# A decoder layer on one core: both heads of a pair transposed in one group of six, their products with the values in the transposes' banks, and the low tiles of w_up 32 bytes further into larger buffers

## The chip, the cores and the metric

One NeuronCore of one Trainium2 chip runs the kernel. The metric is the device time of one execution in microseconds. Of the kernel before there are three such times, 434.8, 435.6 and 436.42, with 435.6 as the median, and one execution that was profiled. "TensorE" is the engine that multiplies matrices (PE in the profile), "VectorE" is DVE, "ScalarE" is ACT, "GpSimd" is POOL, and "SyncE" (SP) issues most of the transfers.

## The reference

One layer of a decoder on 256 rows of width 1024, in float32. One projection feeds three mixers. A keeps, for every query, the keys with the largest index scores and has 6 heads; B has 4 slots, each with three dilated windows that are merged by their softmax denominators; C is block-sparse attention with 6 heads (with 256 rows there is one block, so it is causal attention). Each mixer's output is projected, weighted by a sigmoid gate and summed; then follow an output projection, a layer norm, and a feed-forward part with squared relu beside a gated per-layer embedding (PLE):

```
proj = x @ w_in[i]
...
o_a = dsa_mixer(...)
o_b = dilated_mixer(...)
o_c = moba_mixer(...)
gates = jax.nn.sigmoid(x @ w_gate[i]).reshape(bsz, s_len, N_BRANCH, D_MODEL)
merged = (gates[:, :, 0] * (o_a @ w_br_a[i])
          + gates[:, :, 1] * (o_b @ w_br_b[i])
          + gates[:, :, 2] * (o_c @ w_br_c[i]))
x = layer_norm(ALPHA * x + merged @ w_out[i], ln1_g[i], ln1_b[i])
h = jnp.square(jax.nn.relu(x @ w_up[i])) @ w_down[i]
ple = jax.nn.sigmoid(x @ w_ple_gate[i]) * (p[i] @ w_ple[i])
x = layer_norm(ALPHA * x + h + ple, ln2_g[i], ln2_b[i])
```

## The kernel before

**Split operands.** [...] A product is then three matmuls: high by high, high by low, low by high (`prod`, L136). The class `Weights` streams the weights: SyncE loads a tile of 128 x 1024 into one of five `raw` buffers (L71), ScalarE copies it into a high tile `whi` (L75), and VectorE, for the early weights together with GpSimd, subtracts to get the low tile `wlo` (L79). A `raw` buffer is free for the next transfer when its subtraction is done. `W.get` runs up to four units ahead (`AHEAD`); `W.after` holds units back behind named instructions. Some units of w_out have their two parts in `hT` instead of `whi` and `wlo`.

**Stages of the run** (by the timeline): the index projections until 20 us; projections and the three mixers, B, then C, then A, until about 195; the merge (L570 to L575) and the output projection (`b<-whi,q`, `b<-hT,q`) until 225; the PLE products (`mm<-whi,ph`) until 231, and among them the first layer norm, LN1; the products with w_pg, the gate of PLE, until 256.5; w_up (L693 with the high tiles, L695 with the low ones, 32 units) until 346; w_down until 422, and a second layer norm.

**The mixers.** Heads are worked on in pairs: two pairs of slots in B, three pairs in C, three in A, 16 heads in all. For a pair, `logits` (L274) leaves the scores of two heads in two banks; `head` (or `slots` for B) adds the bias, takes the softmax (L346) and scales the rows (`scale_rows`, L335); `attend` transposes the probabilities of one head on TensorE in three blocks of 128 x 128 (L314) into a bank, splits them into `pt` (ScalarE L315, VectorE behind it), multiplies by the values (L318, L319) into another bank, and adds up four parts into `o`; `pair_out` splits `o` into `op`. Between these steps the list `TASKS` gives TensorE products of the gates (`mm<-xl,whi`, `mm<-xh,whi`, `mm<-xh,wlo`, 256 columns each), so that it has work while the other engines run the softmax.

**What sets the order.** The text of the program is not the order on the engines: a scheduler in the tile framework places each engine's instructions, with priorities and pools of buffers deciding. So an edit in one place can move instructions elsewhere. Every engine then executes its own list in order, and an instruction that waits holds up what is behind it. PSUM has banks: three for `mm`, and five (b0 to b4) that are handed out in fixed turns, by `ps_s` for scores (banks 0, 1, 2), `ps_t` for transposes (3), `ps_v` for the products with values (4), and `ps_a` for everything after.

**LN1.** `ln1` runs for two batches of 128 rows, b = 0 and 1, each in two halves of 512 columns: VectorE adds the residual (L634: `Y<-PL,b`), takes statistics (L611, `BN_STATS`; L616, L617), GpSimd takes the root (L618), VectorE normalizes (L623, L625), TensorE transposes four blocks (L644), and ScalarE (L646) and VectorE (L647) split the result into `x1`. The products with w_pg and w_up read `x1`. The PLE products go to `PL` by ScalarE (L663).

Of the kernel before, what the change touches and what calls it, by code (L numbers as in the profile page):

```python
# [11 lines left out]
F32 = mybir.dt.float32  # L12
F32R = mybir.dt.float32r
ALU = mybir.AluOpType
# [6 lines left out]
S = 256  # L21
# [20 lines left out]
FIRST = 4  # L42
DV = 640
# [6 lines left out]
class Weights:  # L50
# [6 lines left out]

    def add(self, src, n, hi=None, lo=None, stage=None, by="v", urgent=0):
        i = len(self.units)
        self.units.append((src, n, hi, lo, stage, by, urgent))  # L60
        return i

    def _split(self, i):
        nc = self.nc
        src, n, hi, lo, r, by, _ = self.units[i]
        if callable(src):
            r = src()
        else:
            if r is None:
                r = self.raw.tile([128, 1024], F32, name="raw", tag="raw")[:, :n]  # L70
            nc.sync.dma_start(r, src)  # L71
        if hi is None:
            hi = self.part.tile([128, 1024], F32R, name="whi", tag="whi")[:, :n]
            lo = self.part.tile([128, 1024], F32R, name="wlo", tag="wlo")[:, :n]
        nc.scalar.copy(hi, r)  # L75
        cut = ((nc.vector, slice(None)),) if by == "v" else (
            (nc.vector, slice(0, by * n // 1024)), (nc.gpsimd, slice(by * n // 1024, n)))
        for e, c in cut:
            low = e.tensor_tensor(lo[:, c], r[:, c], hi[:, c].bitcast(F32), op=ALU.subtract)  # L79
            if e is nc.gpsimd:  # L80
                self.pool = low.ins
        self.parts[i] = (hi, lo)

    def get(self, i, ahead=AHEAD):
        while self.done <= min(i + ahead, len(self.units) - 1):
            with ExitStack() as held:
                held.enter_context(self.tc.high_priority(offset=self.units[self.done][-1]))
                for ins in self.after:
                    held.enter_context(self.tc.issue_after(ins))
                self._split(self.done)  # L90
            self.done += 1
        return self.parts.pop(i)
# [3 lines left out]
def hybrid_layer(ctx: ExitStack, tc: tile.TileContext, x0, xn, pT, wqk, wva, wvb, wg, wbc, wba,  # L96
# [18 lines left out]

    ps_s, ps_t, ps_v, ps_a = turns((0, 1, 2)), turns((3,)), turns((4,)), turns((0, 1, 3, 2, 4))

# [44 lines left out]

    def add(*a):
        i = n_u[0]
        n_u[0] += 1
        return W.add(*a, by=DV if i < 58 else "v")

# [138 lines left out]
    n_pt = [0]  # L306

    def attend(P, vh, o, h):

        pt = pts[n_pt[0] % 2]  # L310
        n_pt[0] += 1
        t = next(ps_t)
        for c in range(3):
            pe.transpose(t[:, 128 * c:128 * c + 128], P[:, 128 * c:128 * c + 128], ident)  # L314
        act.copy(pt[:, 0], t[:, 0:384])  # L315
        dve.tensor_tensor(pt[:, 1], t[:, 0:384], pt[:, 0].bitcast(F32), op=ALU.subtract)
        v = next(ps_v).rearrange("p (a s) -> p a s", a=2)
        pe.matmul(v, lhsT=V[:, 0, vh], rhs=pt[:, :, 0:256], start=True, stop=False)  # L318
        pe.matmul(v[:, :, 128:256], lhsT=V[:, 1, vh], rhs=pt[:, :, 256:384], start=False,  # L319
                  stop=True)  # L320
        x = wk2.tile([64, 2, S], F32, name="ov", tag="ov")
        act.copy(x, v[64:128])
        dve.tensor_tensor(x, v[0:64], x, op=ALU.add)
        dve.tensor_tensor(o[64 * h:64 * h + 64], x[:, 0], x[:, 1], op=ALU.add)

# [11 lines left out]

    def head(s, t0, t1, vh, o, h):
        e = wk.tile([128, 384], F32, name="e", tag="e")
# [8 lines left out]
        scale_rows(e, den)  # L348
        attend(e, vh, o, h)

    def slots(qs, k, Ts, vh, o):
# [10 lines left out]
        for h in range(2):  # L362
# [9 lines left out]
            scale_rows(e[:, 0], den)  # L372
            attend(e[:, 0], vh + h, o, h)

# [11 lines left out]
    with ExitStack() as begin:  # L386
# [4 lines left out]
        with tc.high_priority(offset=1000):  # L391
# [4 lines left out]
            for k in range(KT):  # L396
# [5 lines left out]
                dve.tensor_tensor(sl[:, k], g0[:, k, S:], sh[:, k].bitcast(F32), op=ALU.subtract)  # L402
        first = [next(ps_s if f < 3 else ps_t)[:, 0:S] for f in range(FIRST)]
        for k in range(KT):
# [65 lines left out]
    for j in range(3):  # L470
        ps = feat(13 + 2 * j)
        k = k_pair(ps)
        q = q_pair(feat(14 + 2 * j))
        s = logits(q, k)
        o = opair()
        for h in range(2):
            n = 2 * j + h
            if n % 3 == 0:
                T = toeplitz(18 + n, 1)
            head(s, T[:, n % 3, 128:256], T[:, n % 3], 5 + n, o, h)  # L480
            fill("g")
        pair_out(o, 5 + j)
# [3 lines left out]
    T = None  # L486
    for j in range(3):
# [3 lines left out]
        for h in range(2):  # L491
# [4 lines left out]
            with tc.issue_after(W.pool):  # L496
                pool.tensor_tensor(ta[:, 0:128], T[:, n % 3, 128:256], am[:, 0:128], op=ALU.add)
                pool.tensor_tensor(ta[:, 128:384], T[:, n % 3], am[:, 128:384], op=ALU.add)
            head(s, ta[:, 0:128], ta[:, 128:384], 0, o, h)
            fill("gg" if n == 0 else "gc")  # L500
# [20 lines left out]
    u_pg = [add(wpg[i], 1024) for i in range(8)]  # L521
    u_up = [[add(wup[i], 1024)] for i in range(32)]

# [67 lines left out]
    w2 = ctx.enter_context(tc.tile_pool(name="w2", bufs=2, reuse_waits="tile"))  # L591
    s2 = ctx.enter_context(tc.tile_pool(name="s2", bufs=4, reuse_waits="tile"))
    Y = p3.tile([128, 2, D], F32, name="Y")
# [370 lines left out]
```

## Time and profile before

| | before |
|---|---|
| median of 3 runs | 435.6 us (434.8 to 436.42) |
| the profiled execution | 437.98 us |
| its span in the trace | 436.2 us |
| TensorE (PE) busy | 425.1 us, 97% of the span |
| VectorE (DVE) busy | 350.5 us, 80% |
| ScalarE (ACT) busy | 276.2 us, 63% |
| GpSimd (POOL) busy | 105.4 us, 24% |

The profile shows one execution. A row of a timeline gives the start in us from the span's beginning, the duration in us, the engine, the source line, the operation, what it writes and reads by the program's names, the shapes and how many alike were put together; in brackets stands the idle time ahead of it and what ended it. Matmuls overlap each other, so that the time from one start to the next, not the duration, is what one of them costs.

### The profile page before, as it was taken

To read this page: it belongs to the slowest core of one execution; us is meant where nothing else is said; L and a number is where in the kernel's file an instruction comes from. 1 tells how busy PE (TensorE), PEld (TensorE's weight loads), DVE (VectorE), ACT (ScalarE), POOL (GpSimd) and SP (SyncE) were. 2 spreads that over 40 slices of the span, in tenths; PEclk is the share of its full clock that TensorE was granted. 3 is DMA by queue.
4 is the path that set the end of the run, shared out by engine and by line. 5 is a ranking of instruction groups with operands and counts; after the bars stand their busy time and mean duration, and the time that the engine had idled before them with its cause. 6 is when DMAs were issued, how large, how long until landed. Compare 5 with 4: busy or idle time off the path is not lost.

```text
span 436.2 us, 7669 instructions
## 1 busy us (share of the span) xinstructions
PE 425.1 (97%) x2799; PEld 386.0 (88%) x2799; DVE 350.5 (80%) x625; ACT 276.2 (63%) x490; POOL 105.4 (24%) x98
## 2 busy tenths in 40 slices
PE   8999999999999999999998999999999999999993
PEld 8999999999999999999886888888888888888882
DVE  5978987577476577879957779999988897998984
ACT  6775375586787777756524567788887855665500
POOL 2563355395434566400000000000100000000001
PEclk9999999999999999999999999999999999999997
DMA  8797756457654436455960875656795377758411
GB/s 298 291 326 234 230 173 191 150 189 250 183 151 145 128 109 187 144 192 178 400 246 0 288 237 185 187 180 203 277 268 187 115 207 269 200 192 278 155 41 57
DMA packets 27690, 86.39 MB, mean 198 GB/s; under 512 B 2884, under 2 KB 6892, under 8 KB 27268
## 3 DMA queue, kind: packets, MB, share of 16 engines
q1 hardware_dynamic: 25872, 79.54, 55.1%
q0 software_dynamic: 640, 2.17, 2.9%
q10 hardware_dynamic: 1140, 4.19, 2.6%
q8 instruction: 22, 0.36, 0.3%
q14 instruction: 16, 0.13, 0.1%
HBM read 83.99 MB, written 1.90 MB: 197 GB/s over the span
## 4 chain that ended last, share of the span: by engine, by line
PE 88%; DVE 5%; issue 3%; DMA 2%; POOL 0%; POOLq 0%; ACT 0%; DVEq 0%; ACTq 0%
PE mm L136 40%; PE b L136 18%; PE mm L693 13%; PE mm L695 7%; PE b L274 3%; PE b L407 3%; DMA raw<-in_wpg_dram 2%; PE b L314 1%; PE b L318 1%; DVE hT L79 1%; DVE st L611 1%; DVE Y L625 1%; PE b L131 1%; DVE G L570 1%; DVE Y L634 1%
## 5 line engine op out<-in xcount | busy, mean ns | idle before, releaser
L79 DVE TENSOR_TENSOR wlo<-raw,whi 128x1024 fp32r<-128x1024 f32 (+5 forms) x146 | 157.5, 1092 | 41.9 <-ACT whi L75 37.9
L75 ACT CAST whi<-raw 128x1024 fp32r<-128x1024 f32 (+3 forms) x146 | 146.1, 1011 | 48.8 <-PE b L136 11.7
L79 POOL TENSOR_TENSOR wlo<-raw,whi 128x384 fp32r<-128x384 f32 (+3 forms) x58 | 78.8, 1367 | 82.6 <-ACT whi L75 73.6
L136 PE MATMUL mm<-xl,whi 128*128 128x256 f32 x336 | 95.7, 285 | 0.0
L136 PE MATMUL mm<-xh,whi 128*128 128x256 f32 x336 | 95.3, 284 | 0.0
L136 PE MATMUL mm<-xh,wlo 128*128 128x256 f32 x336 | 95.0, 283 | 0.0
L136 PEld LDWEIGHTS mm<-xl,whi 128*128 128x128 f32 x336 | 63.3, 188 | 1.0
L693 PE MATMUL mm<-x,whi 128*128 128x512 f32 x256 | 64.1, 392 | 0.0
L136 PEld LDWEIGHTS mm<-xh,whi 128*128 128x128 f32 x336 | 63.3, 188 | 0.7
L136 PEld LDWEIGHTS mm<-xh,wlo 128*128 128x128 f32 x336 | 63.3, 188 | 0.3
L693 PEld LDWEIGHTS mm<-x,whi 128*128 128x128 f32 x256 | 46.1, 189 | 8.3
L136 PE MATMUL b<-whi,hT 128*128 128x512 f32 (+2 forms) x164 | 51.8, 381 | 0.0
L695 PEld LDWEIGHTS mm<-x,wlo 128*128 128x128 f32 x256 | 34.9, 190 | 2.5
L741 POOL DMA_DIRECT2D rows<-in_wdq_dram x4 | 3.6, 972 | 135.3 <-DVE wlo L79 81.9
L695 PE MATMUL mm<-x,wlo 128*128 128x256 f32 x256 | 35.7, 282 | 0.0
L136 PEld LDWEIGHTS b<-whi,hT 128*128 128x128 f32 x164 | 30.5, 188 | 5.8
L136 PE MATMUL b<-wlo,hT 128*128 128x512 f32 (+2 forms) x82 | 31.2, 381 | 0.0
L618 POOL TENSOR_TENSOR rs<-rs,half 128x1 f32<-128x1 f32 x4 | 4.1, 1031 | 103.3 <-DVE rs L617 103.3
L698 DVE TENSOR_REDUCE r<-mm 128x256 f32<-128x512 f32 x32 | 22.0, 688 | 4.9 <-PE mm L695 4.9
L136 PE MATMUL mm<-op,whi 128*128 128x256 f32 x128 | 23.6, 281 | 0.0
L136 PE MATMUL b<-whi,x 128*128 128x512 f32 x64 | 20.4, 394 | 0.0
L241 ACT ACTIVATE G<-mm 128x256 f32<-128x256 f32 x24 | 9.2, 381 | 17.4 <-PE mm L136 17.3
(162 smaller groups left out, 740.0 us busy)
## 6 DMA issues: line engine op xcount, KB each, us to landing
raw<-in_wup_dram SPq DMA_DIRECT2D x32, 512.0 KB
raw<-in_wg_dram SPq DMA_DIRECT2D x24, 512.0 KB
raw<-in_wqk_dram SPq DMA_DIRECT2D x18, 512.0 KB
raw<-in_wdn_dram SPq DMA_DIRECT2D x16, 512.0 KB
raw<-in_wdq_dram SPq DMA_DIRECT2D x12, 512.0 KB
raw<-in_wout_dram SPq DMA_DIRECT2D x8, 512.0 KB
raw<-in_wpg_dram SPq DMA_DIRECT2D x8, 512.0 KB
T<-tabd SPq DMA_DIRECT2D x24, 128.0 KB
```

What stands on the lines that cost most here:

```text
L75: nc.scalar.copy(hi, r)
L79: low = e.tensor_tensor(lo[:, c], r[:, c], hi[:, c].bitcast(F32), op=ALU.subtract)
L131: pe.transpose(t[:, 0:128], ident, ident)
L136: m = pe.matmul(ps, lhsT=a[x], rhs=b[y], start=first and i == 0, stop=last and i == 2)
L241: act.activation(G[:, n_g[0]], ps, AF.Tanh, scale=0.5)
L274: m = pe.matmul(ss[h][:, QC[b]], lhsT=q[d, x, c], rhs=k[d, y, 0:128 * (b + 1)], start=i == 0, stop=i == 2)
L314: pe.transpose(t[:, 128 * c:128 * c + 128], P[:, 128 * c:128 * c + 128], ident)
L318: pe.matmul(v, lhsT=V[:, 0, vh], rhs=pt[:, :, 0:256], start=True, stop=False)
L407: pe.matmul(first[f], lhsT=w[:, k, 128 * f:128 * f + 128], rhs=x[:, k], start=k == i == 0, stop=k == KT - 1 and i == 2)
L693: pe.matmul(ps, lhsT=hi[:, cs[k]], rhs=x1[:, :, k], start=k == 0, stop=False)
L695: pe.matmul(ps[:, :, 0], lhsT=lo[:, cs[k]], rhs=x1[:, :, k, 0], start=False, stop=k == KT - 1)
L698: dve.tensor_reduce(r, ps.rearrange("p b a t -> p b t a"), axis=AX.X, op=ALU.add)
```

## The change

There are four edits. `attend` is called once for each pair, with both heads, and no longer for each head: it first transposes the six blocks, three per head with block 1 first, and `keep_in_program_order` pins the order of all but the first; then it splits and multiplies one head after the other. The second head comes first in the list. The banks 3 and 2 take turns for transposes and also for the products with values, while the scores have banks 0, 1 and 4, and `ps_v` is gone. The low tile of a weight is 1152 elements wide instead of 1024, and the units of w_up start 8 elements (32 bytes) into it (`off=8`). LN1's and LN2's pool of small tiles, `s2`, has two buffers instead of four.

```diff
-    def add(self, src, n, hi=None, lo=None, stage=None, by="v", urgent=0):
+    def add(self, src, n, hi=None, lo=None, stage=None, by="v", urgent=0, off=0):
         i = len(self.units)
-        self.units.append((src, n, hi, lo, stage, by, urgent))
+        self.units.append((src, n, hi, lo, stage, by, urgent, off))
...
-            lo = self.part.tile([128, 1024], F32R, name="wlo", tag="wlo")[:, :n]
+            lo = self.part.tile([128, 1152], F32R, name="wlo", tag="wlo")[:, off:off + n]
...
-    ps_s, ps_t, ps_v, ps_a = turns((0, 1, 2)), turns((3,)), turns((4,)), turns((0, 1, 3, 2, 4))
+    ps_s, ps_t, ps_a = turns((0, 1, 4)), turns((3, 2)), turns((0, 1, 3, 2, 4))
...
-    def attend(P, vh, o, h):
-
-        pt = pts[n_pt[0] % 2]
-        n_pt[0] += 1
-        t = next(ps_t)
-        for c in range(3):
-            pe.transpose(t[:, 128 * c:128 * c + 128], P[:, 128 * c:128 * c + 128], ident)
-        act.copy(pt[:, 0], t[:, 0:384])
-        dve.tensor_tensor(pt[:, 1], t[:, 0:384], pt[:, 0].bitcast(F32), op=ALU.subtract)
-        v = next(ps_v).rearrange("p (a s) -> p a s", a=2)
...
+    def attend(heads, o):
+
+        ts = []
+        for i, (P, vh, h) in enumerate(heads):
+            t = next(ps_t)
+            for c in (1, 2, 0):
+                m = pe.transpose(t[:, 128 * c:128 * c + 128], P[:, 128 * c:128 * c + 128], ident)
+                if i or c != 1:
+                    tc.keep_in_program_order(m)
+            ts.append(t)
+        for t, (P, vh, h) in zip(ts, heads):
+            pt = pts[n_pt[0] % 2]
+            n_pt[0] += 1
+            act.copy(pt[:, 0], t[:, 0:384])
+            dve.tensor_tensor(pt[:, 1], t[:, 0:384], pt[:, 0].bitcast(F32), op=ALU.subtract)
+            v = next(ps_t).rearrange("p (a s) -> p a s", a=2)
...
-    def head(s, t0, t1, vh, o, h):
+    def head(s, t0, t1, h):
...
         scale_rows(e, den)
-        attend(e, vh, o, h)
+        return e
...
-            attend(e[:, 0], vh + h, o, h)
+        attend([(es[h][:, 0], vh + h, h) for h in (1, 0)], o)
...
-            head(s, T[:, n % 3, 128:256], T[:, n % 3], 5 + n, o, h)
+            e = head(s, T[:, n % 3, 128:256], T[:, n % 3], h)
+            heads = [(e, 5 + n, h)] + (heads if h else [])
+            if h:
+                attend(heads, o)
             fill("g")
...
-    u_up = [[add(wup[i], 1024)] for i in range(32)]
+    u_up = [[add(wup[i], 1024, off=8)] for i in range(32)]
...
-    s2 = ctx.enter_context(tc.tile_pool(name="s2", bufs=4, reuse_waits="tile"))
+    s2 = ctx.enter_context(tc.tile_pool(name="s2", bufs=2, reuse_waits="tile"))
```

The change moves instructions at three places. The rows below are the order on an engine, with no time in it; in the changed kernel the line numbers are 6 to 12 higher (L314 stays, L318 is L324, L570 is L582, L571 is L583, L575 is L587, L611 is L623, L616 is L628, L634 is L646, L644 is L656, L646 is L658, L663 is L675, L693 is L705).

The first place is TensorE at the second pair of C. Before, the first head's transposes stand in two pieces among the gate products:

```order
L136 MATMUL mm<-xl,whi 128x256
L314 MATMUL b_1794<-ident,e 128x128
L136 MATMUL mm<-xh,whi 128x256
L136 MATMUL mm<-xh,wlo 128x256
L314 MATMUL b_1794<-ident,e 128x128 x2
```

Further on, its products with the values stand directly ahead of the second head's transposes:

```order
L318 MATMUL b_1800<-pt_116,V 128x512
L319 MATMUL b_1800<-pt_116,V 128x2x128
L314 MATMUL b_1855<-ident,e 128x128 x3
L136 MATMUL mm<-xl,whi 128x256
```

After the change, in the same pair:

```order
L136 MATMUL mm<-xl,whi 128x256
L314 MATMUL b_1842<-ident,e 128x128 x3
L314 MATMUL b_1846<-ident,e 128x128 x3
L136 MATMUL mm<-xh,whi 128x256
L136 MATMUL mm<-xh,wlo 128x256
```

The first head's transposes have moved back to the second head's, and the products with the values of both heads follow later, each among gate products. In the first pair of A the six still stand in two groups, of three and three; in the seven other pairs they are one.

The second place is VectorE at the merge, where `G` holds the gates, `q` the merged rows and `wlo` the low part of a w_out unit. Before:

```order
L570 SCALAR_TENSOR_TENSOR G<-G,mm 128x2x256
L571 TENSOR_TENSOR G<-G 128x2x256
L570 SCALAR_TENSOR_TENSOR G<-G,mm 128x2x256
L575 SCALAR_TENSOR_TENSOR q<-G,q 128x256
L571 TENSOR_TENSOR G<-G 128x2x256
L570 SCALAR_TENSOR_TENSOR G<-G,mm 128x2x256
L575 SCALAR_TENSOR_TENSOR q<-G,q 128x256
L79 TENSOR_TENSOR wlo<-raw,whi 128x1024
```

After:

```order
L582 SCALAR_TENSOR_TENSOR G<-G,mm 128x2x256 x2
L583 TENSOR_TENSOR G<-G 128x2x256 x2
L582 SCALAR_TENSOR_TENSOR G<-G,mm 128x2x256
L587 SCALAR_TENSOR_TENSOR q<-G,q 128x256 x2
L583 TENSOR_TENSOR G<-G 128x2x256
L79 TENSOR_TENSOR wlo<-raw,whi 128x1024
```

The second product of the merge is now used before the first L583, the first `q` comes two operations later, and one more L583 stands ahead of the `wlo`. Some rows later, the third of the four `hT` low parts has two more L587 ahead of it than it had.

The third place is VectorE at the beginning of LN1, where the four `wlo` are those of w_ple (two) and of w_pg's first two units. Before:

```order
L79 TENSOR_TENSOR wlo<-raw,whi 128x1024 x4
L634 SCALAR_TENSOR_TENSOR Y<-PL,b_2936 128x512
L634 SCALAR_TENSOR_TENSOR Y<-PL,b_2937 128x512
L611 BN_STATS st<-Y 128x6 x2
L634 SCALAR_TENSOR_TENSOR Y<-PL,b_2938 128x512
L616 BN_AGGR mv<-st 128x2
```

After:

```order
L79 TENSOR_TENSOR wlo<-raw,whi 128x1024 x3
L646 SCALAR_TENSOR_TENSOR Y<-PL,b_2936 128x512
L646 SCALAR_TENSOR_TENSOR Y<-PL,b_2937 128x512
L623 BN_STATS st<-Y 128x6
L79 TENSOR_TENSOR wlo<-raw,whi 128x1024
L623 BN_STATS st<-Y 128x6
L646 SCALAR_TENSOR_TENSOR Y<-PL,b_2938 128x512
L628 BN_AGGR mv<-st 128x2
```

The fourth `wlo` has moved behind the first batch's two residual sums and one of its statistics. On TensorE, six of the PLE products that stood between the first and the second group of LN1's transposes now stand ahead of both, so that eight transposes follow each other; on ScalarE the last copy of the PLE products (L675) stands ahead of the first cast to `x1` (L658) and no longer behind it. From w_up on, the order is the same on every engine.

More of the change, by code (lines that the diff above doesn't have):

```diff
@@ L64, in _split @@
         nc = self.nc
-        src, n, hi, lo, r, by, _ = self.units[i]
+        src, n, hi, lo, r, by, _, off = self.units[i]
         if callable(src):
@@ L86, in get @@
             with ExitStack() as held:
-                held.enter_context(self.tc.high_priority(offset=self.units[self.done][-1]))
+                held.enter_context(self.tc.high_priority(offset=self.units[self.done][-2]))
                 for ins in self.after:
@@ L161, in hybrid_layer, with add @@
     n_u = [0]
-    def add(*a):
+    def add(*a, off=0):
         i = n_u[0]
         n_u[0] += 1
-        return W.add(*a, by=DV if i < 58 else "v")
+        return W.add(*a, by=DV if i < 58 else "v", off=off)
     G = pm.tile([128, 24, S], F32, name="G")
@@ L306, in hybrid_layer @@
     n_pt = [0]
-    def attend(P, vh, o, h):
-        pt = pts[n_pt[0] % 2]
-        n_pt[0] += 1
-        t = next(ps_t)
-        for c in range(3):
-            pe.transpose(t[:, 128 * c:128 * c + 128], P[:, 128 * c:128 * c + 128], ident)
-        act.copy(pt[:, 0], t[:, 0:384])
-        dve.tensor_tensor(pt[:, 1], t[:, 0:384], pt[:, 0].bitcast(F32), op=ALU.subtract)
-        v = next(ps_v).rearrange("p (a s) -> p a s", a=2)
[L318 to L324, printed above, removed]
+    def attend(heads, o):
[13 more added lines that the diff above has]
+            v = next(ps_t).rearrange("p (a s) -> p a s", a=2)
+            pe.matmul(v, lhsT=V[:, 0, vh], rhs=pt[:, :, 0:256], start=True, stop=False)
+            pe.matmul(v[:, :, 128:256], lhsT=V[:, 1, vh], rhs=pt[:, :, 256:384], start=False,
+                      stop=True)
+            x = wk2.tile([64, 2, S], F32, name="ov", tag="ov")
+            act.copy(x, v[64:128])
+            dve.tensor_tensor(x, v[0:64], x, op=ALU.add)
+            dve.tensor_tensor(o[64 * h:64 * h + 64], x[:, 0], x[:, 1], op=ALU.add)
     def pair_out(o, kt):
@@ L402, in hybrid_layer @@
                 dve.tensor_tensor(sl[:, k], g0[:, k, S:], sh[:, k].bitcast(F32), op=ALU.subtract)
-        first = [next(ps_s if f < 3 else ps_t)[:, 0:S] for f in range(FIRST)]
+        first = [next(p)[:, 0:S] for p in (ps_s, ps_s, ps_s, ps_t)]
         for k in range(KT):
@@ L498, in hybrid_layer @@
                 pool.tensor_tensor(ta[:, 128:384], T[:, n % 3], am[:, 128:384], op=ALU.add)
-            head(s, ta[:, 0:128], ta[:, 128:384], 0, o, h)
+            e = head(s, ta[:, 0:128], ta[:, 128:384], h)
+            heads = [(e, 0, h)] + (heads if h else [])
+            if h:
+                attend(heads, o)
             fill("gg" if n == 0 else "gc")
```

## The prediction

> **What bounds the kernel now.** I read the chain that ended last first, then the waits of TensorE, then the only two places where it waits in the middle of the run.
>
> ```profile
> PE 88%; DVE 5%; issue 3%; DMA 2%; POOL 0%; POOLq 0%; ACT 0%; DVEq 0%; ACTq 0%
> ```
>
> This is section 4 of the page: the chain by engine. TensorE carries 88%. So a microsecond is won where TensorE executes fewer or shorter instructions, or where it waits. The view of waits for TensorE has two rows; one is the start (1.7 us for the identity), the other is this:
>
> ```profile
> PE b L644 <- DVE Y L625: 1.8, 2, 1.3
> ```
>
> L644 transposes the rows that the first LayerNorm (LN1) made. The timeline of TensorE there:
>
> ```profile
> 228.75 0.39 PE L136 MATMUL mm<-whi,pl 128*128 128x512 f32 x1
> 229.59 0.66 PE L644 MATMUL b<-ident,Y 128*128 128x128 f32 x4 [0.45 <-DVE Y L625]
> ...
> 231.83 0.48 PE L136 MATMUL b<-whi,x 128*128 128x512 f32 x1
> 232.15 0.40 PE L136 MATMUL b<-wlo,x 128*128 128x512 f32 x1
> 233.87 0.66 PE L644 MATMUL b<-ident,Y 128*128 128x128 f32 x4 [1.32 <-DVE Y L625]
> ```
>
> A 512-column product takes 0.227 us from start to start (1.81 us for eight, in a row of w_up below). So 228.75 to 229.59 loses 0.84 − 0.23 = 0.61, and 232.15 to 233.87 loses 1.72 − 0.23 = 1.49: **2.10 us** in all. In the mixers (20 to 195 us) TensorE never waits, though the pairs of heads are worked on there; no shortening of their chain of softmax, copy and product can be worth anything there by itself, only a change in what TensorE executes.
>
> **Part 1: the transposes in groups.** The number of transposes is the same (16 heads in 8 pairs, three each) and so is that of the products on values. What changes is how often TensorE turns from products to transposes and back.
>
> ```profile
> 66.64 0.27 PE L314 MATMUL b<-ident,eb 128*128 128x128 f32 x1
> 66.67 0.37 PE L136 MATMUL mm<-xl,whi 128*128 128x256 f32 x1
> 66.87 0.28 PE L136 MATMUL mm<-xh,whi 128*128 128x256 f32 x1
> ...
> 72.43 0.49 PE L314 MATMUL b<-ident,eb 128*128 128x128 f32 x3
> 72.68 0.36 PE L136 MATMUL mm<-xh,whi 128*128 128x256 f32 x1
> 72.88 0.28 PE L136 MATMUL mm<-xh,wlo 128*128 128x256 f32 x1
> ```
>
> A 256-column product alone steps 0.12. The lone transpose with the product behind it takes 66.87 − 66.64 = 0.23, so 0.11 for the transpose; three take 72.88 − 72.43 − 0.12 = 0.33, so 0.11 each too. A turn costs what two decimals can hide, at most 0.02. The order lists have 24 groups of transposes before and 9 after (the first A pair is still split): 15 turns fewer, so 0 to 0.3 us. I take **−0.1**, nearer to the rows' zero.
>
> Does the second head come in time? Where the six stand in one group, they wait for the later head's scaled rows.
>
> ```profile
> 169.01 0.80 ACT L335 ACTIVATE e<-e,r 128x128 f32<-128x128 f32 x2
> ...
> 173.04 0.40 PE L318 MATMUL b<-pt,V 128*128 128x512 f32 x1
> ```
>
> (The first row is ScalarE's, the second TensorE's, both of the second A pair.) The second head's rows are done at 169.81. In the new order the six stand 11 products ahead of the first value product, which puts their start at about 173.04 − 11 × 0.12 − 0.33 = 171.4. The margin is **1.6 us**, the smallest of the eight pairs as far as I followed them. I cost the wait at nothing; the cover is those 1.6 us of gate products. The value products now take turns in the two banks of the transposes; a bank must be read into pt before its value product, but that product needs pt anyway, so no new wait.
>
> **Part 2: LN1, by the moved order on VectorE.** Nothing in the source of LN1 is changed; the orders show that the scheduler places work differently there. VectorE before:
>
> ```profile
> 222.56 1.23 DVE L79 TENSOR_TENSOR wlo<-raw,whi 128x1024 fp32r<-128x1024 f32 x1 [4.90 <-ACT whi L75]
> 223.70 1.28 DVE L634 SCALAR_TENSOR_TENSOR Y<-PL,b 128x512 f32<-128x512 f32 x2
> 224.90 1.28 DVE L611 BATCH_NORM_STATS2 st<-Y 128x6 f32<-128x512 f32 x2
> 226.09 0.67 DVE L634 SCALAR_TENSOR_TENSOR Y<-PL,b 128x512 f32<-128x512 f32 x1
> ```
>
> VectorE sat idle for 4.90 us in front of a wlo that waited for a weight of w_pg, with LN1's first sums behind it. After, three of the four operations between 223.70 and 226.09 stand ahead of that wlo. They need two sums of the out-projection; from the first product on q (203.07, below) the later one ends after 48 + 31 products of 0.227, at 221.0, so the three fit before 222.56. What follows in LN1 comes 3/4 × 2.39 = **1.79 us earlier**, and with it the last transposes' rows: 233.87 − 1.79 = 232.1.
>
> TensorE is then bound by itself: six PLE products now precede the first transposes (228.75 + 7 × 0.227 = 230.34), eight transposes follow as one block (8 × 0.11, to 231.2), and ScalarE must copy them before the gate's products on x:
>
> ```profile
> 230.34 0.59 ACT L646 CAST x<-b 128x512 fp32r<-128x512 f32 x1 [0.57 <-PE b L644]
> 231.68 0.60 ACT L663 ACTIVATE PL<-mm 128x512 f32<-128x512 f32 x1 [0.75 <-PE mm L136]
> ```
>
> After, the L663 copy stands ahead of the L646 one: 230.5 + 0.60 + 0.59 = 231.7, then two products as in the rows of 231.83 and 232.15 (0.32 + 0.23): 232.3. So the gain is at most 233.87 − 232.3 = **1.6**.
>
> Against it stands the weight itself:
>
> ```profile
> 212.47 8.91 DMA raw<-in_wpg_dram
> ...
> 256.55 1.81 PE mm L693 x8
> 258.36 0.95 PE mm L695 x8
> 259.31 1.84 PE mm L693 x8
> ```
>
> In the chain, the transfer that this wlo needs was issued at 212.47, when an L79 of hT (the last VectorE piece ahead of it) had freed its buffer, and took 8.91 us. That release moves. VectorE in the merges:
>
> ```profile
> 199.32 0.69 DVE L571 TENSOR_TENSOR G<-G 128x512 f32<-128x512 f32 x1
> 199.94 0.68 DVE L570 SCALAR_TENSOR_TENSOR G<-G,mm 128x512 f32<-128x512 f32 x1
> 200.53 0.42 DVE L575 SCALAR_TENSOR_TENSOR q<-G,q 128x256 fp32r<-128x256 f32 x1
> 200.87 0.68 DVE L571 TENSOR_TENSOR G<-G 128x512 f32<-128x512 f32 x1
> ```
>
> After, the second L570 comes before the first L571; its products may not be there until 199.9, a gap of up to 0.62. And the third hT's L79 has two more L575 (0.34 each) ahead of it. The release is late by 0 (if no gap, and the queue evens out) to 0.62 + 0.68 = 1.3 us; behind it on SyncE's queue stand the other weights of w_pg. I take 0.8 as a middle. Then the last transposes start at 232.1 + 0.8 = 232.9, and **LN1 gains 1.0** (bounds 0.5 and 1.6). The merges themselves have cover: from 199.94, four of these steps of 0.6 (L570, two L571, L570) and an L575 of 0.42 have q's first tile done by about 202.8 instead of 200.95, and TensorE wants it here:
>
> ```profile
> 203.07 0.40 PE L136 MATMUL b<-whi,q 128*128 128x512 f32 x1
> ```
>
> So 0.3 us of cover are left; were it gone, each 0.1 later would cost 0.1.
>
> **Part 3: 32 bytes.** In the built programs x1 and both weight tiles begin at multiples of 64 bytes; after, only w_up's wlo stands 32 bytes off. The rows of w_up above: 0.95 for eight low products is 0.119 each, while half of a 512-column step is 0.113; and the high group takes 1.81 when no low group precedes it, 1.84 otherwise. If all that went, it were 256 × 0.0063 + 31 × 0.03 = 2.5 us. Nearest rows where moving operand and weights already stand 32 bytes apart, gates first, then the branches' projections:
>
> ```profile
> 114.31 0.28 PE L136 MATMUL mm<-xl,whi 128*128 128x256 f32 x1
> ...
> 118.57 0.28 PE L136 MATMUL mm<-xl,whi 128*128 128x256 f32 x1
> ```
>
> ```profile
> 191.92 6.67 PE mm L136 x57
> ```
>
> The first stretch is 36 steps: 4.26/36 = 0.1183. The other: 6.67/57 = 0.1170. By these a low product would gain 0.0010 to 0.0023, times 256: 0.3 to 0.6. I take **−0.4**, with 0 and −2.5 as bounds. A loss could only come through VectorE, which writes wlo:
>
> ```profile
> 256.50:346.00 89.50, 89.50 (x515) 78.76 (x514) 82.15 (x119) 71.16 (x127) 1.86 (x2) 1.00 0.65 201
> ```
>
> This row of the windows has VectorE busy for 82.15 of w_up's 89.50 us, while TensorE is never idle; 7.35 us over 32 tiles cover a write slower by 0.23 each. The two buffers fewer for LN1's small tiles cost nothing: LN1 has two batches, one each.
>
> [...] The 0.119 beside 0.113 shows that something is paid, not that it hangs on addresses; no run so far shows which.
>
> **Sum.** −1.0 − 0.4 − 0.1 = −1.5. The profiled execution took 437.98 us (span 436.2), so its like would take 436.5. That execution lies 2.4 above the median of the three runs, 435.6; the same difference from the median gives **434.1 us**.
>
> **Rivals.**
> - The shift does nothing (20%). For it: the gates, already 32 bytes apart, step 0.1183, hardly below 0.1194. Against: the projections' 0.1170. Result: −1.1, **434.5**.
> - The shift frees w_up's low products wholly (13%). For it: unlike the gates' and the projections', their two operands start on the same offset, and of the three they are the slowest. Against: the gates' rows. −1.1 − 2.5 = −3.6: **432.0**.
> - The transfer of w_pg eats LN1's gain (12%). It does so when it lands 1.8 us later or more, which 1.3 of release plus a worse place among the other transfers could give: TensorE then waits as before. −0.5: **435.1**.
> - Other side: the six wait for the second head at every pair (10%). TensorE then stands still, with the gate products queued behind the transposes that could have filled the time. It decides from 1.6 us of lateness; each 0.1 beyond it costs 0.1 at each of eight pairs. With 0.5 beyond it: 8 × 0.5 = +4.0, with the −1.4 of the other parts +2.6: **438.2**. Against it: the 1.6 us at the tightest pair, and that TensorE's list of waits before has no L314 in it at all. It would come about if the second head's rows, which stand behind whole weight copies on ScalarE (169.01 follows one), fell behind one or two more of them.
>
> **How the numbers follow.** The forecast holds 45%. Low end: LN1 −1.6, the transposes −0.3 and w_up −2.5 would be 431.2; all three at once is unlikely, so 431.8. High end: the transfer's rival at 435.1, plus the 0.8 by which the highest run of before stands above the median, plus 0.5 for the beginning of the waiting six at one or two pairs: 436.4. What is left out is that rival's body and the tails, under 2 in 10. Half a per cent, 2.2 us, is about what a measurement of this kernel can tell from no change: faster needs below 433.4, which are the freed products and a good quarter of the forecast's own spread (0.13 + 0.13 + 0.02); slower needs above 437.8, the waiting six: 0.10. The rest, 0.62, is the same.
>
> **What would show it.** LN1: the two waits of L656 (the old L644) on Y drop from 1.8 us to below 1.0, with one place left. w_pg: the fourth wlo's start, 222.56 before, moves to about 223.4; beyond 224.3 the gain is gone. w_up: eight low products at 0.93 to 0.94 instead of 0.95; 0.91 is the rival, 0.95 the other. Mixers: no wait of L314; one at most pairs makes the forecast wrong, as would a wait on q in front of 203.07. Their stretch should end about 0.1 us sooner.

## The result, and the profile after

The changed kernel is **slower**, by 0.8%: 438.97 us as the median of nine runs (436.46 to 440.18) against 435.43 for the kernel before (434.8 to 436.42, nine runs); the ratio is 1.0078, with a 95% interval of 1.0059 to 1.0097. The forecast was 434.1, in a range of 431.8 to 436.4. A second series gave 439.17 (435.85 to 441.66) against 435.72, ratio 1.0067 (1.0040 to 1.0094).

| | before, first trace | before, second trace | after, first trace | after, second trace |
|---|---|---|---|---|
| time of this execution | 437.98 | 435.63 | 436.46 | 438.23 |
| span | 436.2 | 433.8 | 434.7 | 436.4 |
| TensorE (PE) busy | 425.1 | 424.4 | 424.0 | 425.0 |
| VectorE (DVE) busy | 350.5 | 352.6 | 355.2 | 354.9 |

The first thing to see is that neither first trace stands for its kernel: that of before lies 2.5 us above its median, that of after 2.5 below. Compared with each other they show 1.5 us in favour of the change, the very number that I forecast. So I took further traces, and compare stages by when TensorE starts certain work, all worked out from rows of the timelines. "Mixers" is from the first index scores to the first product on q of the output projection; "LN1" from there to the first product of w_up:

| execution (time) | mixers | LN1 stretch |
|---|---|---|
| before, first (437.98) | 178.23 | 53.32 |
| before, second (435.63) | 178.16 | 50.92 |
| after, first (436.46) | 179.37 | 51.45 |
| after, second (438.23) | 179.87 | 51.80 |
| after, third (438.22) | 179.28 | 52.71 |

Two places differ: the mixers are 1.1 to 1.7 us longer after the change, and the LN1 stretch is 0.5 to 1.8 longer than in the second trace of before, though shorter than in the first. In all, the first trace of after is only 0.8 longer than the second of before, although these two stretches are 1.7 longer: its index scores began 0.8 earlier (at 24.20 instead of 25.00), which is luck.

The waits of TensorE in the first trace of after, beside the 1.7 us for the identity at the start that both kernels have (engine, line, who ended the wait: us in total, times, longest):

```profile
PE b L274 <- DVE q L218: 1.0, 1, 1.0
PE b L136 <- ACT x L658: 0.3, 1, 0.3
```

And all of them in the second trace of before:

```profile
PE b L131 <- POOL ident masks.py:199: 1.7, 1, 1.7
PE b L407 <- ACT sh L400: 0.2, 1, 0.2
```

The 2.1 us of LN1 waits, on which the forecast's largest term rested, are not there in an execution at the median (nor in the traces of the four edited versions of the kernel before, further down). And there is a wait that the kernel before never had: the scores of the first C pair (L274) wait for q. The chain of work that ended last, in the first trace of after, says from what (start, us, what):

```profile
94.73 0.66 PE b L314 x6
95.38 1.15 PE mm L136 x10
96.53 4.99 DMA pr<-in_pT_dram
...
101.55 0.63 ACT ph L472
...
102.21 0.69 DVE pl L473
102.90 1.20 DVE ov L329 x2
104.10 0.34 DVE k L229
...
104.46 0.43 DVE o L330
...
104.91 1.12 DVE o L330
106.04 0.73 DVE wlo L79
106.77 0.09 DVE op L334
...
107.03 0.42 DVE q L218
...
107.50 0.95 PE b L274 x12
```

`pr` is the load of the per-layer input p, which the mixers don't need at all. It goes into one of the two buffers of B's probabilities (`eb`), that of the last B pair's first head, and this buffer is free when that head's three transposes are done. Before, they ended at 94.4, while the second head's followed at 99.7; after, they are the last of the six, done at 95.4. ScalarE (`ph`) and VectorE (`pl`) then stand at the load, for 3.62 and 2.45 us, and q stands behind them in both lists. Before the change, VectorE's own timeline at this place read:

```profile
101.36 0.69 DVE L467 TENSOR_TENSOR pl<-pr,ph 128x512 fp32r<-128x512 f32 x1 [2.22 <-ACT ph L466]
101.97 0.68 DVE L323 TENSOR_TENSOR ov<-b,ov 64x512 f32<-64x512 f32 x1
102.58 0.54 DVE L316 TENSOR_TENSOR pt<-b,pt 128x384 fp32r<-128x384 f32 x1
103.04 0.41 DVE L229 TENSOR_TENSOR k<-mm,k 128x256 fp32r<-128x256 f32 x1
103.37 0.41 DVE L324 TENSOR_TENSOR o<-ov 64x256 f32<-64x256 f32 x1
103.71 0.82 DVE L79 TENSOR_TENSOR wlo<-raw,whi 128x640 fp32r<-128x640 f32 x1
104.44 0.42 DVE L218 SCALAR_TENSOR_TENSOR q<-mm,q 128x256 fp32r<-128x256 f32 x1
```

The engines stood at p then too (ScalarE for 2.48 us, and VectorE behind it for 2.22), and from pl to q it took 3.08 us; it takes 4.82 after, since both heads' `ov` and `o` now come together, and `op` ahead of q. q was done at 104.86, and the scores started at 106.59: 1.7 us to spare, which no row of waits shows. The change used up 1.0 (the later issue of p) and 1.7 (the longer way to q).

In SyncE's queue the later issue reads so, before:

```profile
95.12 0.33 SPq L71 DMA_DIRECT2D raw<-in_wg_dram  x1
95.54 0.38 SPq L465 DMA_DIRECT2D pr<-in_pT_dram  x1
```

and after, where the load of p has fallen behind a second weight:

```profile
94.55 1.89 SPq L71 DMA_DIRECT2D raw<-in_wg_dram  x2
96.53 0.38 SPq L471 DMA_DIRECT2D pr<-in_pT_dram  x1
```

It is the transposes that set the time and not the second weight: in both traces the load is issued 1.2 us after those three have ended.

The theory for the first half of the loss: **q comes late because two in-order engines stand at the late p**. For the second half, LN1: the second weight of w_pg arrives late in every trace of the changed kernel, and its low part now stands among LN1's own operations on VectorE. The rivals: the six wait for the second head; the wider tiles cost; the new order of q and op.

### The profile page after: what moved, and what is told of

Read it like the earlier page. It is cut to its first block, busy times and chain, and to the rows that moved or that the text cites. A ratio compares the mean times of both kernels' runs of the same rounds, so it can differ in the third digit from the quotient of the medians.

```text
span 434.7 us, 7675 instructions
## 1 busy us (share of the span) xinstructions
PE 424.0 (98%) x2799; PEld 384.8 (89%) x2799; DVE 355.2 (82%) x625; ACT 274.6 (63%) x490; POOL 107.4 (25%) x98
## 4 chain that ended last, share of the span: by engine, by line
PE 94%; DMA 2%; DVE 2%; ACT 1%; POOLq 0%; issue 0%; SPq 0%; DVEq 0%
PE mm L136 40%; PE b L136 25%; PE mm L705 14%; PE mm L707 7%; PE b L274 3%; PE b L413 2%; DMA G<-in_x_dram 1%; PE b L314 1%; DMA pr<-in_pT_dram 1%; PE b L324 1%; PE b L325 0%; DVE o L330 0%; DVE ov L329 0%; POOLq L972 0%; DVE Y L637 0%; PE b L656 0%
## 5 line engine op out<-in xcount | busy, mean ns | idle before, releaser
L705 PE MATMUL mm<-x,whi 128*128 128x512 f32 x256 | 64.2, 393 | 0.0
L705 PEld LDWEIGHTS mm<-x,whi 128*128 128x128 f32 x256 | 45.8, 188 | 8.3
```

What stands on the lines that cost most here:

```text
L705: pe.matmul(ps, lhsT=hi[:, cs[k]], rhs=x1[:, :, k], start=k == 0, stop=False)
```

## The experiments

**Both kernels again.** The second and third traces above, without an edit.

> The kernel before, unchanged, for a second trace. Its nine times lie within 434.8 to 436.42, and the profiled execution of 437.98 above all of them. If the 2.1 us of waits in LN1 belong to every execution, they stand in this trace too at about 435.5 + 2.4. If they were that one execution's, this trace has under 1 us of waits in LN1 and a time near 435.5; then the 1.0 us that I counted for LN1 was never to be had in the median.

> The changed kernel, unchanged, for a second trace. Its nine times spread over 3.7 us (436.46 to 440.18), the trace in hand is the fastest of them and has one new wait: 1.0 us of TensorE at the first C pair (scores L274 wait for q), behind the load of p, which landed at 101.5 instead of 100.7. Theory p: the slower executions have a longer wait at that place, 1 us + (time - 436.5), and nothing else. Rival six: the slower executions have waits of L314 at several pairs. Median 439.0 in both.

before_again: 435.64 (435.39 to 437.35, 11 runs), no wait in LN1, so the first trace of before was the exception. after_again: 439.17, with a wait on q of 1.6 and 0.6 more in two other places. No trace of the changed kernel has a wait of L314: the second head always came in time. The expectation that the wait alone makes the long times was too simple, as the halved clock below shows.

**The grouping without the 32 bytes.**

```diff
-            lo = self.part.tile([128, 1152], F32R, name="wlo", tag="wlo")[:, off:off + n]
+            lo = self.part.tile([128, 1024], F32R, name="wlo", tag="wlo")[:, :n]
...
-    u_up = [[add(wup[i], 1024, off=8)] for i in range(32)]
+    u_up = [[add(wup[i], 1024)] for i in range(32)]
...
-    s2 = ctx.enter_context(tc.tile_pool(name="s2", bufs=2, reuse_waits="tile"))
+    s2 = ctx.enter_context(tc.tile_pool(name="s2", bufs=4, reuse_waits="tile"))
```

> The changed kernel without the 32 bytes, with low tiles of 1024 and four small buffers as before; the order is that of the changed kernel on every engine. Theory p and rival six: as the changed kernel, 438.5 to 439. Rival shift: 435 to 436. If w_up's 32 bytes are worth 0.4 as I forecast, this is 0.4 slower than the changed kernel; by the trace in hand (89.24 to 89.16 us in w_up) 0.1.

438.55 (438.1 to 440.92), ratio 1.0067 (1.0043 to 1.0091): the whole loss stays without the 32 bytes, so it belongs to the grouping, with the banks and the orders that came with it.

**The 32 bytes without the grouping**: the same lines the other way round, in the kernel before.

> The kernel before with low tiles of 1152, w_up's 32 bytes in, and two small buffers instead of four; the order is that of before on every engine. My forecast had 0.4 for this: 435.3. By the traces of w_up in hand (89.24 us before, 89.16 after) 0.1: 435.6, not to be told from before.

435.68, ratio 0.9997 (0.9984 to 1.0009): no difference that can be told. Yet the trace can: the 512 products of w_up take 89.24 us from first to last start in both traces of before and with the grouping alone, 89.16 wherever the 32 bytes are. From the start of a low group to that of the next high one, a low product costs 0.1183 on average instead of 0.1191, a high one likewise 0.2304 instead of 0.2300. Inside a low group the step is 0.1189 in both; what changes is mostly the turns, from low to high (0.1146 instead of 0.1200) and from high to low (0.2335 instead of 0.2267). The chain of shift_only there:

```profile
262.59 1.86 PE mm L693 x8
264.44 0.95 PE mm L695 x8
265.39 1.83 PE mm L693 x8
267.22 0.94 PE mm L695 x8
```

A high and a low group take 2.80 and 2.78 in turn, where before it was 2.79 each time: what is won at one turn is mostly lost at the other.

**p loaded early, its split too early.** First try to take p out of the way, in the changed kernel:

```diff
-        tab, gone = (pm.tile([N_BIAS, N_U], F32, name=n) for n in ("tab", "gone"))
+        tabs = pm.tile([128, 2 * N_U], F32, name="tabs")
+        tab, gone = tabs[0:N_BIAS, 0:N_U], tabs[0:N_BIAS, N_U:]
+        early.append(tabs)
...
-    pr = wk2.tile([128, 2, S], F32, name="pr", tag="eb")
+    pr = early[0][:, 0:2 * S].rearrange("p (a s) -> p a s", a=2)
     nc.sync.dma_start(pr, pT)
```

> The changed kernel, with the input p loaded into the space of the bias tables, which is free early, instead of one of the two buffers of slots (eb) that the last slots' transposes release. Theory p: the wait at the first C pair goes and the spread with it: 434 to 435.5. Rival six (TensorE waits for the second head): still 438 to 439, with the wide spread. Rival shift (the wider low tiles cost): still 438 to 439.

446.5 (445.05 to 452.19): a miss, and an instructive one. Without the buffer to wait for, the scheduler put the load at 44.88 and the split right behind it, ahead of the weights' casts. ScalarE then stood 11.7 us at p, the weights behind it came late, and TensorE waited 8.7 us for a q of the first B pair. The place moved, the mechanism is the same: an in-order engine at a load that nobody needs yet.

**p loaded early, its split where it was.** As above, with the split pinned behind the last slots' pt copies:

```diff
-    act.copy(ph, pr)
-    dve.tensor_tensor(pl, pr, ph.bitcast(F32), op=ALU.subtract)
+    with tc.issue_after(split[0]), tc.issue_after(split[1]):
+        act.copy(ph, pr)
+        dve.tensor_tensor(pl, pr, ph.bitcast(F32), op=ALU.subtract)
```

(`split` holds the copy to `pt` and the subtraction behind it.)

> The changed kernel with p loaded early into the space of the bias tables, as before, but with its split (ph, pl) left where it stood, behind the last slots' pt copies; the order is otherwise that of the changed kernel but for a handful of rows. The earlier try had moved the split up too, and ScalarE stood 11.7 us at it. Theory p (the load's buffer is released later by the grouped transposes, and the first C pair's q is late by it): the 1.0 to 1.6 us wait of the scores on q goes, so 1.3 to 2.5 us below the changed kernel of this batch, about 437. Rival order (q is late because ScalarE's list now has op, waiting for o, ahead of q): at least half of the wait stays, 438 to 439.

437.3 (435.42 to 440.87), ratio 1.0037 (1.0016 to 1.0058). The wait on q is gone, and the mixers take 178.20 us, between the two traces of before (178.16, 178.23). So the whole loss in the mixers of this trace was p, and the grouped transposes by themselves are worth nothing measurable there. (Two of the 12 runs, 440.87 and 439.33, still have a granted clock of 0.991, a sign that is explained below; no trace shows what happened in them.)

**The load as late as ever, its split behind q.** In the changed kernel:

```diff
-    pr = wk2.tile([128, 2, S], F32, name="pr", tag="eb")
-    nc.sync.dma_start(pr, pT)
-    act.copy(ph, pr)
-    dve.tensor_tensor(pl, pr, ph.bitcast(F32), op=ALU.subtract)
...
         q = q_pair(feat(14 + 2 * j))
+        if j == 0:
+            with tc.issue_after(last[0]), tc.issue_after(low[0]):
+                pr = wk2.tile([128, 2, S], F32, name="pr", tag="eb")
+                nc.sync.dma_start(pr, pT)
+                act.copy(ph, pr)
+                dve.tensor_tensor(pl, pr, ph.bitcast(F32), op=ALU.subtract)
```

> The changed kernel with the load of p where it was (same buffer, same lateness), but its split (ph on ScalarE, pl on VectorE) moved behind the first C pair's q; otherwise the order stays but for two rows. Theory: it is not the late load that costs but that two in-order engines stand at it with q behind them. Then the wait on q goes as with p in a space of its own: 436.8 to 437.6, and no run at a granted clock of 0.991 or less. Rival: something else of the grouping makes q late; then 438 to 439 and a third of the runs at 0.991 or less, as with the changed kernel (8 of 21).

437.79 (436.57 to 439.5), a little above the 436.8 to 437.6 that was expected; no run is at a clock of 0.991 or less. No wait on q, mixers 178.26 us, with the load issued at 97.16, later than in the first trace of after. So the late load costs nothing where nobody stands at it.

**q ahead of op**, with p in front as it was:

```diff
-        pair_out(o, 3 + j)
+        if j == 0:
+            pair_out(o, 3)
         fill("g")
+    late = o
...
         q = q_pair(feat(14 + 2 * j))
+        if j == 0:
+            with tc.issue_after(last[0]), tc.issue_after(low[0]):
+                pair_out(late, 4)
```

> The changed kernel with q and op of the first C pair swapped on ScalarE and on VectorE, so that q no longer stands behind op there; the two o sums stay ahead of it. VectorE's op is 0.33 us, so the wait on q falls by about 0.33 to 0.5 us; p stays in front. Expected 438.0 to 438.7, little below the changed kernel's 439, with fewer runs at a clock of 0.991 or less. If the order of q and op were the main cause: 437 or less.

437.66 (436.14 to 441.58): more than the 0.33 us of VectorE's op explains. The wait on q is still there in the trace, 0.8 us, with p landing 5.0 us after its issue as in the first trace of after (1.0): a cut of 0.2 there. Part of the rest lies in the distribution: one run in twelve has a granted clock of 0.991 or less, where the changed kernel has 8 of 21; what that means is next. But the other eleven runs too have a median of 437.4, against 438.2 for the other 13 of the changed kernel, and no trace shows where that comes from.

**What the long waits set off.** The trace of the changed kernel with LN1's rows late (below) happened to be a bad one, 442.48 us. TensorE there:

```profile
108.03 0.28 PE L137 MATMUL mm<-xl,whi 128*128 128x256 f32 x1
110.33 1.65 PE L275 MATMUL b<-k,q 64*128 64x128 f32 x12 [2.02 <-DVE q L219]
111.91 0.58 PE L137 MATMUL mm<-xh,whi 128*128 128x256 f32 x1
```

The wait on q is 2.0 us, because p took 6.6 us to land (97.78 to 104.39), and the twelve scores behind it take 1.65 us instead of 0.95. The windows of this trace (from:to, length, busy us of PE, PEld, DVE, ACT, POOL, then the granted clock, the share of DMA and GB/s):

```profile
104.00:107.00 3.00, 3.00 (x26) 2.86 (x25) 1.95 (x4) 2.56 (x5) 0.00 (x0) 1.00 0.24 96
107.00:110.00 3.00, 1.05 (x7) 0.78 (x6) 2.94 (x6) 1.55 (x4) 1.06 (x1) 0.95 0.02 5
110.00:113.00 3.00, 2.67 (x17) 2.45 (x18) 2.32 (x4) 1.75 (x3) 2.40 (x2) 0.50 0.60 175
113.00:116.00 3.00, 3.00 (x16) 3.00 (x16) 1.36 (x10) 2.55 (x10) 0.79 (x1) 0.50 0.64 210
116.00:119.00 3.00, 3.00 (x25) 3.00 (x25) 0.83 (x1) 2.02 (x4) 1.46 (x1) 0.91 0.39 139
```

The granted clock falls to **0.50** while TensorE still waits (taken as one step from 1.00, the mean of 0.95 up to 110 puts the fall at 109.7) and stays there until a little after 116. From these scores to those of the next C pair it takes 15.01 us, with p in a space of its own 12.37: the clock costs another 2.6 us. The length of a wait alone doesn't decide: here the clock fell, by that estimate, 1.4 us after the end of the last product, with 0.25 idle just ahead, while a wait of 1.6 in the second trace of after, and four of 0.6 to 1.0 in other traces, kept it at 1.00 in every window from 104 to 119. The mean granted clock of each run hints at how often that happens: the six runs of after_p_early, whose trace has the wait of 8.7, are at 0.980 to 0.987; 8 of the 21 runs of the changed kernel in its first two series are at 0.991 or less, with a median of 440.1, while the other 13 have 438.2. None of the 110 runs of the kernel before beside all the series is below 0.992. That is a thin line, and only this one trace shows the fall itself.

> The changed kernel for a third trace. Theory: the wait on q at the first C pair between 1 and 2.5 us; where it is over about 2 us the granted clock falls to 0.5 for some 6 us behind it, as in the trace with the rows late (wait 2.0, clock 0.50 from 110 to 116), and the time is 439.5 or more; where it is under, the clock stays and the time is 436 to 438.5.

438.22, with a wait on q of 0.9, and the clock at 1.00 from 104 to 119: it agrees with the lower half of the expectation. Its time is made up of that wait, 1.2 us of waits in LN1 (0.9 and 0.3) and 0.8 at the start, so a time of 438 can come without a lost clock.

**LN1's rows later.** What else lands late is the second weight of w_pg. ScalarE's cast of it in the second trace of before:

```profile
217.01 1.06 ACT L75 CAST whi<-raw 128x1024 fp32r<-128x1024 f32 x1 [0.21 <-DMA raw<-in_wpg_dram]
```

and of after:

```profile
214.69 0.34 ACTq L610 DMA_DIRECT2D rows<-in_lnrow_dram  x1
...
223.66 1.06 ACT L75 CAST whi<-raw 128x1024 fp32r<-128x1024 f32 x1 [4.34 <-DMA raw<-in_wpg_dram]
```

It was issued at 212.56 and at 215.60. The 1 MB of LN1's gains and biases ("rows") was issued 0.7 after it in the first case and 0.9 ahead of it in the second. The weight took 4.5 us and 8.1 until its cast. In the changed kernel I put the rows one cast later:

```diff
         act.dma_start(PL, xn)
-        row_load(rows1, 0)
...
+        if b == c == 0:
+            with tc.issue_after(W.his[u_ple[1]]):
+                row_load(rows1, 0)
```

(`W.his` holds ScalarE's cast of each unit.)

> The changed kernel with LN1's gain rows (1 MB) loaded behind ScalarE's second w_ple cast, one later than now; LN1's order thereby falls back to that of before. Theory race: in five traces the second w_pg weight landed within 4.5 us where it was issued ahead of these rows (217.0 in the second trace of before) and 8 to 9 us after its issue where the rows went first (all traces of the changed kernel). Then here it lands early, LN1 takes as long as in the second trace of before, and the time falls by 0.9, to about 438.2. Rival: the weight is late in any case because its release is 1.3 us later; then 439 as the changed kernel.

437.22 (436.32 to 442.73), ratio 1.0051 (1.0025 to 1.0078), 2.0 below the changed kernel and twice what I expected. p is untouched, and 5 of the 12 runs are still at a clock of 0.99 or less.

The edit does two things, however: it moves the rows, and with them VectorE's list in LN1 falls back to the order of before, where the fourth `wlo` stands ahead of the first sums. That order matters too. In the second trace of before:

```profile
214.29 5.03 DVE L79 TENSOR_TENSOR wlo<-raw,whi 128x1024 fp32r<-128x1024 f32 x4
220.43 1.28 DVE L634 SCALAR_TENSOR_TENSOR Y<-PL,b 128x512 f32<-128x512 f32 x2 [1.10 <-PE b L136]
...
224.30 1.41 DVE L623 SCALAR_TENSOR_TENSOR Y<-Y,mv,rows 128x512 f32<-128x512 f32 x2
```

and in the first of after:

```profile
221.01 1.37 DVE L646 SCALAR_TENSOR_TENSOR Y<-PL,b 128x512 f32<-128x512 f32 x2 [2.03 <-PE b L136]
...
222.98 1.23 DVE L79 TENSOR_TENSOR wlo<-raw,whi 128x1024 fp32r<-128x1024 f32 x1
...
226.10 1.40 DVE L635 SCALAR_TENSOR_TENSOR Y<-Y,mv,rows 128x512 f32<-128x512 f32 x2
```

From the first sum to the first normalization (`Y<-Y,mv,rows`) it takes 3.88 us before and 5.09 after. The `wlo` inside makes 1.2 of that, although in this trace VectorE did not stand at its weight (0.01 us); in the seven other traces with this order it waited 0.35 to 1.23 more there. Wherever the first normalization comes later than in the second trace of before (counted from the first product on q), the LN1 stretch is longer by that delay less 0.8 us, in all 13 such traces of the 16 that were taken. So the moved `wlo` alone, with first sums 0.2 later, makes the 0.5 of the first trace of after, and the late weight the rest, up to 1.8. The new order with an early weight was not tried.

Both edits together, p's and this one:

> Both edits together in the changed kernel. If the late p and the lost race are all that the change costs, 435.0 to 436.0, as the kernel before, with the narrow spread. If something else in the grouping costs (waits for the second head, more turns), 437 or more.

435.66 (434.71 to 439.18), ratio **1.0004 (0.9986 to 1.0022)**: with p out of the way and the rows late, the changed kernel is as fast as the one before. The parts nearly add up: 439.2 − 437.3 = 1.9 for p, 439.2 − 437.2 = 2.0 for the rows, 3.5 for both. What the rows' edit gains stands in the medians alone. The trace of after_rows_late has the weight 6.4 us under way and an LN1 stretch of 51.89, no better than the changed kernel's. The trace of after_both fell on one of its two high runs (437.64), with the weight late in spite of all, and the waits of the first trace of before:

```profile
PE b L666 <- DVE Y L644: 1.8, 2, 1.3
```

The rows' edit alone in the kernel before:

> The kernel before with the rows one cast later; nothing else moves. Theory race: the runs of before at 437 to 438 (3 of 23) are those in which the rows went first by a tenth of a us, as in the first trace (rows 212.39, weight 212.47); here there are none of them: median 435.5, highest below 436.5. Rival: the high runs have other causes and stay.

435.23 (434.95 to 436.18), ratio 0.9989 (0.9977 to 1.0000); no run above 437, of which the kernel before has 4 in the 35 runs beside it. In its trace the weight took 6.8 us, with the rows issued 4.3 behind it, and the LN1 stretch is 51.12.

And the rows earlier there, ahead of the cast of the first w_ple unit:

```diff
-                for ins in self.after:
+                for ins in self.after + tuple(self.pin.get(self.done, ())):
...
-        row_load(rows1, 0)
+        W.pin[u_ple[0]] = (row_load(rows1, 0).ins,)
```

> The kernel before with LN1's rows loaded one ScalarE cast earlier than now, so that they go about 1.5 us ahead of the second w_pg weight; VectorE's order, and so the weight's release, stays that of before. If the rows ahead of the weight make it land 8 to 9 us after its issue: a wait of 1.5 to 2.1 us in LN1 in most runs, 437.2 to 437.9. If it is the later release that makes the weight late in the changed kernel: 435.7.

436.27 (435.73 to 437.83), ratio 1.0017 (1.0002 to 1.0031): neither. The rows went 1.5 us ahead of the weight, which took 6.9 us and was cast at 219.39. VectorE waited 2.56 us for that cast and began LN1's first sum at 221.62, 1.2 later than in the second trace of before (220.43), and the LN1 stretch is 51.21, only 0.3 longer: LN1 has most of that to spare. In seven traces of the changed kernel's order the weight was issued at 213.5 to 215.6, 0.1 to 1.1 behind the rows, was 7.7 to 9.0 us under way and was cast after 221.7, which is too late for LN1. What makes it late is not settled. The later release is not needed: in the first trace of before the weight, issued at 212.47 and 0.1 behind the rows, took 9.0. Nor does it take the rows ahead: with the rows 0.7 or more behind it, the weight took 3.9 to 4.5 us in three traces, and 6.4 to 7.8 in three others (after_rows_late, before_rows_late, after_both).

Last, p's split behind q and the rows late, in the kernel before:

> The kernel before with p's split behind q and LN1's rows one cast later. In before q has 1.7 us to spare, so the first edit is worth nothing by itself in most runs; the second took the runs above 437 away. 435.0 to 435.4, highest below 436.3. If before lost time at p in some runs, 434.8 or less.

435.7 (434.86 to 436.28), ratio 0.9993 (0.9982 to 1.0005): both edits in the kernel before, and above the 435.0 to 435.4 expected. Its mixers had slack at p, and taking p out of the way brings nothing. Of all versions, before_rows_late has the lowest median, and its interval ends at 1.0000; a version that clearly beats both kernels was not found.

## Why the prediction was wrong, point by point

- "**In the mixers TensorE never waits**", and "I cost the wait at nothing; the cover is those 1.6 us of gate products": this step failed. I followed what the transposes feed (pt, the value products), and found rightly that the second head comes in time: no trace has a wait of L314, and the rival that was slower, the six waiting at every pair, did not happen, although its 438.2 lies near the time measured. What I did not follow is what the transposes release. The buffer of the last B pair goes to p, two engines stand at p with q behind them, and q had 1.7 us to spare, which the change spent. No view of waits lists such slack; it stood in the distance between q's end (104.86) and the scores (106.59).
- "**LN1 gains 1.0**": the mechanism that I read was right for the execution that I read it from. There LN1 waited 2.1, the three operations did move ahead of the weight's wlo, and the first trace of after has 51.45 against 53.32 in that stretch. At one and the same lateness of the weight's cast (18.3 us behind the first product on q, in the first trace of after and in that of after_both, which has the old order) the new order has its first normalization 1.8 us earlier, the 1.79 of my working. But the late weight was that execution's own. The second trace of before has 50.92 without a wait, so that there was nothing to gain at the median, and there the same move is a cost: the `wlo` of 1.2 us that used to be done ahead of LN1 now stands inside it. My counter-term, the release up to 1.3 us later, did come: 212.47 to 214.17, with the first product on q moved by 0.5, is 1.2.
- "The same difference from the median gives 434.1": this carried the error. An execution 2.4 us above the median should have been asked which of its waits the median doesn't have.
- "**w_up −0.4**": 0.1 measured, none in the time. By the gates' row, 0.1183, I had 0.3 for the low products; they came to 0.1183 with their turns counted in, for 0.2, and the high ones gave 0.1 back. The place changes an average step by 0.8 ns, and the 32 bytes alone leave the time where it was (435.68, ratio 0.9997): for this part the rival (the shift does nothing) was the better forecast.
- "**Transposes −0.1**": with p out of the way the mixers take 178.20 and 178.26 against 178.16 and 178.23: nothing.

In place of my sum: p about +1.9, of which the wait itself is 0.6 to 1.6 in the traces at full clock, and the halved clock, in some runs, probably the rest; LN1 +0.5 to +1.8 in the traces, 1.6 to 2.0 by the medians with and without the rows' edit; the 32 bytes and the grouped transposes themselves 0. That the forecast of the waiting six lay so near is chance.

## What to carry to other kernels

Where an edit makes a tile live longer, ask who gets its buffer next, which engine stands at that load in order, and what is behind it there. Slack is read as the distance from an operand's end to its use, not from a list of waits, and an edit that moves many small things should be weighed against the smallest such distance. And before a wait in one profile is counted as a gain, compare that execution's time with the median: a wait that only this execution has cannot be saved in the others. An operation that waits for a load is best moved behind other work when the load is late (p's split behind q: 437.79 against 439.17); when it comes in time, it only stands in the way there (the moved `wlo`, with 0.01 us of waiting: 5.09 us from LN1's first sum to its first normalization, against 3.88).

## What I had not expected of the hardware

A wait of 2.0 us on TensorE, with 0.25 just ahead of it, cost 2.6 us more than itself, since the granted clock stood at 0.50 for about 6 us behind it, while waits of 0.6 to 1.6 us left it at 1.00 in five traces. And one and the same 512 KB load, the second weight of w_pg, took between 3.9 (before_p_rows) and 9.0 us (first trace of before) from its issue to its cast, which moved LN1 in two traces of the unchanged kernel by 2.4 us.
